# First norm of a two-layer hybrid block on one core: modulation in four blocks of 256 columns, rows of w_in loaded and split with them

## The chip, the cores and the metric

The kernel runs on one core of a Trainium2 chip, in float32, as one launch. The metric is the device time of that core in microseconds. The engines named below are TensorE (PE; its weight loads are listed as PEld), VectorE (DVE), ScalarE (ACT), GpSimd (POOL) and SyncE (SP), which issues most DMA transfers.

## The reference

One inference step of two layers over 128 context tokens and 256 latent tokens (384 together) of width 1024. Each layer modulates a normed input, feeds one wide input projection, mixes tokens in three branches (attention, gated linear attention, pooling), merges them and ends with a gated feed-forward part. What matters here is the start of the first layer:

```python
def _layer(x, cvec, p, ctx):
    mod = (jax.nn.silu(cvec) @ p['w_mod'] + p['b_mod']).reshape(-1, 1, 6 * D_MODEL)
    sh1, sc1, g1, sh2, sc2, g2 = jnp.split(mod, 6, axis=-1)
    hn = _rmsnorm(x, p['g_norm1']) * (1 + sc1) + sh1
    mix, new = _mixer(hn, p, ctx)          # begins with z = hn @ p['w_in']
    ...
```

`cvec` is one vector for the context tokens (c_ctx) and one for the latent tokens (c). The normed input `hn` can't be formed for a column before `sh1` and `sc1` of that column are known, and these need the first 2048 columns of `w_mod` (1024 x 6144): 8 MB.

## The kernel before, in words

All activations lie transposed: a tile `x[n]` holds channels 128 n to 128 n + 127 on the partitions and the 384 tokens along the row. `hn` is kept as two parts of reduced precision, `hh` and `hl`; each weight tile is likewise split into `wh` (a ScalarE copy, L151) and `wl` (a subtraction on VectorE, L155), and a product takes three matmuls, wh with hh, wh with hl, and wl with hh.

The order of work is written out by hand. `unit` (L100) lists every weight load; `seg` (L106) lists pieces of work with the units they use. `run` (L166) goes through the pieces, and before each one `pump` (L122) issues the next loads, strictly in the order of the list, as far as there is room: loads of w_mod go to tiles m0 to m5, m10 and m11 (each free again once its products are issued), loads of w_in to a ring of four tiles `raw`, free again once their split is done. `pump` also splits loaded tiles, in order, up to a limit `split_lim` and while fewer than three split pairs are held. The instructions of each engine run in the order in which they are issued.

`plan_start` (L331) writes the start of layer 0. It goes over n = 0 to 7, the eight column blocks of 128. For block n two loads of w_mod come, one for the shift columns and one for the scale columns (`w_cols`, L1178 to L1182: 1024 rows x 128 columns, runs of 512 B, 512 KB), and after block n + 1 the load of row n of w_in (`rows`, L1190 to L1195: 128 rows x 512 columns, 256 KB), so that rows 6 and 7 follow the last block. The stages s run from 0 to 9:

- `mod` (L350): 8 small matmuls for each of the two loads. The two conditioning vectors are the stationary operand (32 columns wide, of which two are used); four groups of 32 PSUM partitions each take two of the eight row blocks.
- `copy` (L359): ScalarE takes the partial sums out of PSUM. It also sets `split_lim`, so that row s - 1 may be split from stage s on.
- `post` for block s - 1: two transposes (L373), a sum over the four groups (L377), the bias (L380), the scale (L381), and `hn`: the modulated norm of that block. Even blocks do it on VectorE (L656), ScalarE (L674) and VectorE (L680), odd blocks on VectorE (L656), ScalarE (L664, L670) and POOL (L671).
- `row_fn` for row s - 2: twelve matmuls (L1242 to L1244) that add row block s - 2 of the product of w_in's 512 query and key columns of the gated branch. With row 7 come 32 small matmuls of the gate columns (L1231, weights `glw`) and the evacuations (L1246).

In between stand `bcast` (the norm's factor, L365, L367), `x_rest` (the last transposes of x, L322), `load_gl` (the load of `glw` on POOL's queue, L587), `prep_vec`, and in stage 6 `begin` (named `started_fn`): a POOL memset of a tile (L1200) and eight small loads of w_gate into it on SyncE (L1204). That tile is first used by the matmuls of L726, in the middle of the first tile of the next part. The next part (`tile_seg`, matmuls at L219) goes through the columns of w_in in tiles of 1024 x 128.

Of the kernel before, what the change touches and what calls it, by code (L numbers as in the profile page):

```python
# [10 lines left out]
AF = mybir.ActivationFunctionType  # L11
ALU = mybir.AluOpType
AX = mybir.AxisListType

D = 1024
KT = D // 128
# [11 lines left out]
V_BMOD, V_N1, V_N2, V_PS, V_GLA, V_QN, V_KN, V_BG, NV = 0, 48, 56, 64, 68, 69, 70, 71, 75  # L28


class Kern:
# [299 lines left out]
    def plan_start(self, rows, row_fn):  # L331

        nc, a = self.nc, self.a
        st = {}
        w_mod = a["w_mod"][0]
        um, ur = {}, {}
        for n in range(KT + 1):
            if n < KT:
                um[n] = [self.unit(("mod0", n, v), self.w_cols(w_mod, v * D + n * 128), 0,
                                   (0, 1, 2, 3, 4, 5, 10, 11)[(2 * n + v) % 8]) for v in range(2)]  # L340
            if n:
                ur[n - 1] = rows(n - 1)

        def mod(u, n, v):
            if v == 0:
                st[n] = self.psa()
            ps = st[n]
            for k in range(KT):
                j = k % 4
                nc.tensor.matmul(ps[32 * j:32 * j + 32, v * 128:v * 128 + 128], self.sc[:, k, :],  # L350
                                 self.raw[u][:, k * 128:k * 128 + 128], start=k < 4, stop=k >= 4,
                                 tile_position=(0, 32 * j))

        def copy(n):
            self.split_lim = ur[n - 1] + 1 if 0 < n <= KT else 0 if n == 0 else 1 << 30
            if n >= KT:
                return
            raw = self.t(("kn", "KA")[n % 2], [128, 256])
            nc.scalar.activation(raw, st[n][:, 0:256], AF.Copy)  # L359
            st[n] = raw  # L360

        def bcast():
            self.prep_vec(0, 0)
            ps = self.psa()
            nc.tensor.matmul(ps[:, 0:T], self.ones(), self.dg0)  # L365
            self.rs0 = self.t("ssq", [128, T])
            nc.vector.tensor_copy(self.rs0, ps[:, 0:T])  # L367

        def post(n):
            raw = st.pop(n)  # L370
            pt = self.psa()
            for v in range(2):
                nc.tensor.transpose(pt[:, v * 128:v * 128 + 128], raw[:, v * 128:v * 128 + 128], self.ident)  # L373
            m = self.modT[0]
            ab = m[:, n:n + 9:8, :]
            src = pt[:, 0:256].rearrange("p (v j c) -> p v c j", v=2, j=4)[:, :, 0:2, :]
            nc.vector.tensor_reduce(ab, src, axis=AX.X, op=ALU.add)  # L377
            vec = self.vec[0]
            bm = vec[:, V_BMOD + n:V_BMOD + n + 9:8]
            nc.vector.tensor_tensor(ab, ab, bm.unsqueeze(2).to_broadcast([128, 2, 2]), op=ALU.add)  # L380
            nc.vector.tensor_scalar(m[:, 8 + n], m[:, 8 + n], 1.0, vec[:, V_N1 + n:V_N1 + n + 1],  # L381
                                    op0=ALU.add, op1=ALU.mult)
            self.hn(0, n, 8, 0, self.rs0)

        self.modfin[0, 0] = self.modfin[0, 1] = iter(())
        for s in range(KT + 2):
            if s < KT:
                for v in range(2):
                    self.seg([um[s][v]], lambda u, s=s, v=v: mod(u, s, v), 0)
            self.seg([], lambda s=s: copy(s), 0)  # L390
            if s == 0:
                self.seg([], bcast, 0)
            if 1 <= s <= KT:
                self.seg([], lambda s=s: post(s - 1), 0)
            if s == 1:
                self.seg([], self.x_rest, 0)
            if s == 4:
                self.seg([], lambda: self.load_gl(0), 0)
            if s == 4:
                self.seg([], lambda: self.prep_vec(0, 1), 0)  # L400
            if s == 6:
                self.seg([], self.started_fn, 0)
            if s >= 2:
                self.seg([ur[s - 2]], lambda u, s=s: row_fn(u, s - 2))

    def setup(self):
        nc, a, t = self.nc, self.a, self.t
# [212 lines left out]
    def post(self, out, ps, rs, bb, scale=1.0):  # L620

        nc = self.nc
        nc.vector.tensor_scalar(bb, ps[:, T:T + 2], scale, None, op0=ALU.mult)
        nc.vector.scalar_tensor_tensor(out=out, in0=ps[:, 0:T], scalar=scale, in1=rs, op0=ALU.mult, op1=ALU.mult)  # L624

        def rest():
            for v, (c0, c1) in enumerate(SEG):
                nc.scalar.activation(out[:, c0:c1], out[:, c0:c1], AF.Identity, bias=bb[:, v:v + 1])
        return rest
# [554 lines left out]
    def plan_layer(self, l):  # L1184
        nc, a = self.nc, self.a
        st = {}
# [3 lines left out]
        def rows(k):  # L1190

            def dma(tl):
                ks = slice(k * 128, k * 128 + 128)
                nc.sync.dma_start(tl[:, 0:512], w_in[ks, C_QB:C_QB + 512])
            return self.unit((l, "row", k), dma, 512)  # L1195
# [19 lines left out]
        def row_fn(u, k):  # L1215
            if k == 0:
                st["z"] = [self.pd() for _ in range(3)] + [
                    self.psa(hold=True), self.psa(hold=True) if l else self.p("m")]
            if k == KT - 1:
                st["qbkb"] = self.mid(1, [128, 4, T])  # L1220
                st["q"] = self.mid(0, [128, 4, T])
            h, lo = self.wt[u]
            W = T + 2 if l else T
            hh, hl = (self.hhw, self.hlw) if l else (self.hh, self.hl)
            for g0 in (0, 4) if k == (2 if l else KT - 1) else ():

                ps = st["z"][0]
                for z, x in enumerate((hh, hl)):
                    for g in range(4):
                        kk = g0 + g  # L1230
                        nc.tensor.matmul(ps[32 * g:32 * g + 32, 0:W], self.glw[:, kk, :],  # L1231
                                         x[kk].bitcast(F32),
                                         start=kk == g and z == 0, stop=kk > g and z == 1, tile_position=(0, 32 * g))
            if k == KT - 1:
                if l:
                    bb = st["bb"]
                else:
                    nc.scalar.activation(st["gl"], st["z"][0][:, 0:T], AF.Copy)
            for i, c in enumerate((2, 3, 0, 1)):
                ps = st["z"][i + 1][:, 0:W]  # L1240
                cs = slice(c * 128, c * 128 + 128)
                nc.tensor.matmul(ps, h[:, cs], hh[k], start=k == 0, stop=False)  # L1242
                nc.tensor.matmul(ps, h[:, cs], hl[k], start=False, stop=False)
                nc.tensor.matmul(ps, lo[:, cs], hh[k], start=False, stop=k == KT - 1)  # L1244
                if k == KT - 1 and l == 0:
                    nc.scalar.activation(st["qbkb"][:, c, :], ps, AF.Copy, scale=0.125 if c < 2 else 1.0)  # L1246
                if i == 1:
                    if l and k == 2:
                        st["rs"] = next(st["norm"])
                    self.tick()  # L1250
                    self.run_low()
            if l:
                if k == 0:
                    st["norm"] = self.norm()
                    next(st["norm"])
                if k == 2:
                    begin()
                self.hn_after(k, 2, l, 8, 0, st.get("rs"))
                if k == 6:
                    st["bb"] = bb = self.t("rsmall", [128, 5, 2])  # L1260
                    st["rest"] = self.post(st["gl"], st["z"][0], st["rs"], bb[:, 4])
                if k == KT - 1:
                    st["rest"]()
                    for i, c in ((2, 0), (3, 1), (0, 2), (1, 3)):
                        self.post(st["qbkb"][:, c, :], st["z"][i + 1], st["rs"], bb[:, c], 0.125 if c < 2 else 1.0)()
            if k == KT - 1:
                if l:
                    self.sa_i = next(i for i in range(4) if i not in self.held and (i - 1) % 4 in self.held)
                self.held.clear()
                if l == 0:  # L1270
                    self.spawn(self.setup())
                st["gla"] = self.spawn(self.gla_all(l, st))
# [4 lines left out]
        else:  # L1277
            for k in range(KT):
                u = rows(k)
# [463 lines left out]
```

## Time and profile before

| | us |
|---|---|
| median of 3 runs | 1326.35 (1326.03 to 1326.6) |
| the profiled execution | 1326.22 |
| its span, first to last instruction | 1324.4 |
| TensorE busy | 1291.9 |
| VectorE busy | 852.9 |
| ScalarE busy | 596.1 |

The profile is of one execution. Times in it count from the start of its span; 1.8 us of the execution's time lie outside the span. The span is cut here at two places: until 43.27 us the loads of w_mod come in, and at 54.30 us the first matmul of L219 starts. A clock of 1.00 is the granted TensorE clock as a share of 2.4 GHz.

### The profile page before, as it was taken

The numbers are of one execution on the slowest core, as the hardware profiler recorded it, in microseconds if no ns is written. First come the engines' busy times: TensorE is split into PE (matmuls) and PEld (weight loads), VectorE is DVE, ScalarE is ACT, GpSimd is POOL, SyncE is SP. The second block draws the span as 40 slices with busy tenths as digits, with TensorE's granted clock in tenths as the row PEclk, the third lists the DMA queues.
The fourth block names the chain that finished last, engine by engine and source line by source line (L and its number), as shares of the span: only waits on it lengthen the run. The fifth ranks groups of instructions, "written<-read, shape, count | busy, mean of one in ns | idle before, by whom it ended". The sixth has DMA issues, their size and how long they took to land.

```text
span 1324.4 us, 23404 instructions
## 1 busy us (share of the span) xinstructions
PE 1291.9 (98%) x9285; PEld 1201.2 (91%) x9285; DVE 852.9 (64%) x1522; ACT 596.1 (45%) x1102; POOL 139.7 (11%) x190
## 2 busy tenths in 40 slices
PE   7999999999999999999999999999999999999998
PEld 5797788889998999999988887888999899999998
DVE  4497876454568768676877888754556787544432
ACT  5655455343366333333446646543435643333221
POOL 1142000010033000000222400001102300000000
PEclk9999999999999999999999999999999999999999
DMA  9943545556444656665645545355444266444442
GB/s 288 248 118 98 146 127 143 156 134 199 135 127 115 192 173 198 184 198 166 201 129 151 149 114 142 114 166 139 111 127 128 84 201 189 135 126 123 134 127 61
DMA packets 297788, 198.51 MB, mean 150 GB/s; under 512 B 24560, under 2 KB 282384, under 8 KB 297680
## 3 DMA queue, kind: packets, MB, share of 16 engines
q1 hardware_dynamic: 296928, 196.68, 52.7%
q8 instruction: 73, 1.20, 0.4%
q0 software_dynamic: 608, 0.28, 0.1%
q14 instruction: 35, 0.29, 0.1%
q10 hardware_dynamic: 144, 0.07, 0.0%
HBM read 194.64 MB, written 2.36 MB: 149 GB/s over the span
## 4 chain that ended last, share of the span: by engine, by line
PE 87%; DVE 6%; DMA 2%; issue 2%; SPq 1%; ACT 1%; POOL 1%; ACTq 0%; POOLq 0%; DVEq 0%
PE d L219 65%; PE d L1429 7%; PE d L1361 2%; DMA m<-in_w_mod_dram 2%; PE m L472 1%; PE s L1120 1%; PE s L1109 1%; PE s L1074 1%; DVE wl L155 1%; PE s L762 1%; DVE nm L1080 1%; PE s L949 1%; SPq L1181 1%; DVE ev L656 1%; PE s L943 1%
## 5 line engine op out<-in xcount | busy, mean ns | idle before, releaser
L155 DVE TENSOR_TENSOR wl<-raw,wh 128x1024 fp32r<-128x1024 f32 (+2 forms) x274 | 328.5, 1202 | 126.3 <-ACT wh L151 122.2
L151 ACT ACTIVATE wh<-raw 128x1024 fp32r<-128x1024 f32 (+2 forms) x276 | 280.0, 1017 | 172.6 <-PE d L219 63.6
L219 PE MATMUL d<-hl,wh 128*128 128x384 f32 x1248 | 252.9, 341 | 0.0
L219 PE MATMUL d<-hh,wh 128*128 128x384 f32 x1248 | 248.2, 342 | 2.0 <-DVE vf L624 2.0
L219 PE MATMUL d<-hh,wl 128*128 128x384 f32 x1248 | 243.0, 338 | 0.0
L219 PEld LDWEIGHTS d<-hh,wh 128*128 128x128 f32 x1248 | 216.0, 189 | 16.9 <-issue 10.9
L219 PEld LDWEIGHTS d<-hl,wh 128*128 128x128 f32 x1248 | 218.2, 189 | 2.0 <-issue 0.3
L219 PEld LDWEIGHTS d<-hh,wl 128*128 128x128 f32 x1248 | 219.8, 189 | 0.0
L219 PE MATMUL d<-m,wh 128*128 128x384 f32 x896 | 166.0, 337 | 0.0
L219 PEld LDWEIGHTS d<-m,wh 128*128 128x128 f32 x896 | 155.7, 188 | 0.4 <-issue 0.4
L251 ACT ACTIVATE m<-tt 128x384 fp32r<-128x384 f32 x60 | 31.3, 525 | 157.4 <-DVE tt L1531 125.7
L219 PE MATMUL d<-m,wl 128*128 128x384 f32 x448 | 87.5, 337 | 0.0
L219 PEld LDWEIGHTS d<-m,wl 128*128 128x128 f32 x448 | 78.6, 188 | 0.0
L1429 PE MATMUL d<-m,wh 128*128 128x384 f32 x384 | 72.2, 341 | 0.0
L1429 PEld LDWEIGHTS d<-m,wh 128*128 128x128 f32 x384 | 66.0, 188 | 6.6 <-issue 5.8
L710 DVE SCALAR_TENSOR_TENSOR x<-d,modT,x 128x128 f32<-128x128 f32 x64 | 23.6, 413 | 53.9 <-PE d L219 46.1
L1412 ACT ACTIVATE tt<-d 128x384 f32<-128x384 f32 x48 | 23.6, 491 | 72.4 <-PE d L219 62.5
L1449 POOL TENSOR_TENSOR m<-m,tt 128x384 f32<-128x384 f32 x16 | 16.9, 1081 | 368.7 <-DVE tt L1447 368.7
L561 POOL TENSOR_TENSOR ssq<-ssq,ev 128x384 f32<-128x384 f32 x18 | 29.4, 1636 | 248.9 <-ACT ev L559 248.9
L1531 DVE TENSOR_TENSOR tt<-tt,d 128x384 f32<-128x384 f32 x42 | 23.2, 554 | 48.9 <-PE d L219 48.6
L1518 ACT ACTIVATE tt<-d 128x384 f32<-128x384 f32 x42 | 20.6, 490 | 67.1 <-PE d L219 63.2
L1110 ACT ACTIVATE pT<-s 128x384 f32<-128x384 f32 (+1 forms) x48 | 20.1, 418 | 60.5 <-PE s L1109 60.5
(319 smaller groups left out, 1607.2 us busy)
## 6 DMA issues: line engine op xcount, KB each, us to landing
raw<-in_w_mod_dram SPq DMA_DIRECT2D x80, 512.0 KB, 3.8
raw<-in_w_in_dram SPq DMA_DIRECT2D x76, 512.0 KB, 4.0
raw<-in_w_ff_gate_dram SPq DMA_DIRECT2D x44, 512.0 KB, 4.8
raw<-in_w_ff_up_dram SPq DMA_DIRECT2D x44, 512.0 KB, 4.6
raw<-in_w_ff_down_dram SPq DMA_DIRECT2D x32, 448.0 KB, 4.4
m<-in_w_mod_dram SPq DMA_DIRECT2D x16, 512.0 KB, 7.1
raw<-in_w_in_dram SPq DMA_DIRECT2D x32, 256.0 KB, 3.9
raw<-in_w_out_dram SPq DMA_DIRECT2D x16, 512.0 KB, 4.0
```

What stands on the lines that cost most here:

```text
L151: nc.scalar.activation(h[:, f], w[:, f], AF.Copy)
L155: e.tensor_tensor(l[:, f], w[:, f], h[:, f].bitcast(F32), op=ALU.subtract)
L219: nc.tensor.matmul(ps, w[:, k * width + col:k * width + col + 128], xs[xi](k0 + k), start=first and n == 0, stop=last and n == tot - 1)
L251: self.nc.scalar.activation(h, v, AF.Copy)
L561: e.tensor_tensor(self.ssq, self.ssq, sq, op=ALU.add)
L710: nc.vector.scalar_tensor_tensor(out=self.x[n][:, c0:c1], in0=ps[:, c0:c1], scalar=self.modT[l][:, fg + n, v:v + 1], in1=self.x[n][:, c0:c ...
L1110: nc.scalar.activation(pTs[u // 2][:, v, 0:nk * 128], ps[:, 0:nk * 128], AF.Copy)
L1361: nc.tensor.matmul(vps[c], (self.hl if z else self.hh)[kk][:, c * 128:c * 128 + 128], w[:, k * 512:k * 512 + 512], start=kk == 0 and w is ...
L1412: nc.scalar.activation(tt, ps[:, 0:T], AF.Tanh, scale=0.5)
L1429: nc.tensor.matmul(ps[i], w[:, k * 256 + i * 128:k * 256 + i * 128 + 128], x2[xi](k), start=w is h and xi == 0 and k == 0, stop=w is lo an ...
L1518: nc.scalar.activation(tt, pg, AF.Tanh, scale=0.5)
L1531: nc.vector.tensor_tensor(tt, tt, pu, op=ALU.mult)
```

## The change

The eight column blocks of 128 become four of 256. For each block there are four loads of w_mod: shift and scale, each as the upper and the lower 512 rows, 512 rows x 256 columns (runs of 1 KB, 512 KB each as before). `mod` has four matmuls of 256 columns for each load. The rows of w_in come in pairs: for block 0 behind its fourth load, for the other blocks ahead of their fourth load. `split_lim` is set to include the pair of block s after the third load's products of that block, while the pair's own products come in stage s + 1. `copy` writes one tile of 512 columns. `post(s)` comes in its own stage s: four transposes, two reductions, one bias add and one scale over both column blocks, then `hn` twice. In stages 1 to 4 the products of row 2s - 2 come ahead of `post(s)` and those of row 2s - 1 behind it. `x_rest` moves into block 0, `load_gl` to stage 1, `prep_vec` to stage 2, `begin` to stage 3 (behind `post(3)`). The gate columns' products are done in two halves, with rows 5 and 7.

```diff
+        for s in range(NB):
+            def two_rows():
+                for n in (2 * s, 2 * s + 1):
+                    ur[n] = rows(n)
+            for i in range(4):
+                if s and i == 3:
+                    two_rows()
+                v, h = i // 2, i % 2
+                um[s, i] = self.unit(("mod0", s, i), self.w_cols(w_mod, v * D + s * 256, nk=4, k0=4 * h, width=256), 0,
+                                     (0, 1, 2, 3, 4, 5, 10, 11)[(4 * s + i) % 8])
+            if not s:
+                two_rows()
...
+            for j in range(4):
+                nc.tensor.matmul(ps[32 * j:32 * j + 32, v * 256:v * 256 + 256], self.sc[:, 4 * h + j, :],
+                                 self.raw[u][:, j * 256:j * 256 + 256], start=h == 0, stop=h == 1,
                                  tile_position=(0, 32 * j))
...
+            if s and i == 2:
+                self.split_lim = ur[2 * s + 1] + 1
...
+        def copy(s):
+            raw = self.t("pT", [128, 512], bufs=2)
+            nc.scalar.activation(raw, st[s], AF.Copy)
+            st[s] = raw
+            if s == 0:
+                self.split_lim = ur[1] + 1
...
+            for b in range(4):
+                nc.tensor.transpose(pt[:, b * 128:b * 128 + 128], raw[:, b * 128:b * 128 + 128], self.ident)
+            m, vec = self.modT[0], self.vec[0]
+            n = 2 * s
             for v in range(2):
...
+                src = pt[:, v * 256:v * 256 + 256].rearrange("p (h j c) -> p h c j", h=2, j=4)[:, :, 0:2, :]
+                nc.vector.tensor_reduce(m[:, 8 * v + n:8 * v + n + 2, :], src, axis=AX.X, op=ALU.add)
...
+            for h in range(2):
+                self.hn(0, n + h, 8, 0, self.rs0)
...
-        for s in range(KT + 2):
-            if s < KT:
-                for v in range(2):
-                    self.seg([um[s][v]], lambda u, s=s, v=v: mod(u, s, v), 0)
-            self.seg([], lambda s=s: copy(s), 0)
+        for s in range(NB + 1):
+            if s < NB:
+                for i in range(4):
+                    self.seg([um[s, i]], lambda u, s=s, i=i: mod(u, s, i), 0)
+                    if (s, i) == (0, 1):
+                        self.seg([], self.x_rest, 0)
+                self.seg([], lambda s=s: copy(s), 0)
             if s == 0:
                 self.seg([], bcast, 0)
-            if 1 <= s <= KT:
-                self.seg([], lambda s=s: post(s - 1), 0)
+            else:
+                self.seg([ur[2 * s - 2]], lambda u, s=s: row_fn(u, 2 * s - 2))
+            if s < NB:
+                self.seg([], lambda s=s: post(s), 0)
             if s == 1:
-                self.seg([], self.x_rest, 0)
-            if s == 4:
                 self.seg([], lambda: self.load_gl(0), 0)
-            if s == 4:
+            if s == 2:
                 self.seg([], lambda: self.prep_vec(0, 1), 0)
-            if s == 6:
+            if s == 3:
                 self.seg([], self.started_fn, 0)
-            if s >= 2:
-                self.seg([ur[s - 2]], lambda u, s=s: row_fn(u, s - 2))
+                self.seg([], free_split, 0)
+            if s:
+                self.seg([ur[2 * s - 1]], lambda u, s=s: row_fn(u, 2 * s - 1))
...
-            for g0 in (0, 4) if k == (2 if l else KT - 1) else ():
+            for g0 in ((0, 4) if l and k == 2 else (0,) if not l and k == 5 else (4,) if not l and k == KT - 1 else ()):
```

`free_split` sets `split_lim` to no limit.

## Rows read from the trace of the kernel before

**Rows 1.** The page: busy us, share of the span, instructions by engine.

```profile
PE 1291.9 (98%) x9285; PEld 1201.2 (91%) x9285; DVE 852.9 (64%) x1522; ACT 596.1 (45%) x1102; POOL 139.7 (11%) x190
```

**Rows 2.** Chain of waits at 35 us: start us, us, what.

```profile
34.85 8.38 DMA m<-in_w_mod_dram
...
43.27 0.65 PE s L350 x16
```

**Rows 3.** Waits, 8 to 52 us: engine, line waited for, total us, times, longest.

```profile
PE s L350 <- DMA m<-in_w_mod_dram: 6.1, 7, 1.8
```

**Rows 4.** Timeline of SyncE's issues: start us, us, queue, line, tiles, count.

```profile
36.50 2.57 SPq L1194 DMA_DIRECT2D raw<-in_w_in_dram  x2
...
43.28 5.39 SPq L1204 DMA_DIRECT2D m<-in_w_gate_dram  x8
```

**Rows 5.** Windows: length, busy PE PEld DVE ACT POOL, clock, DMA share, GB/s.

```profile
4.00:7.00 3.00, 1.64 (x8) 1.44 (x9) 0.01 (x1) 2.50 (x5) 2.34 (x13) 1.00 1.03 387
10.00:12.00 2.00, 1.30 (x21) 0.86 (x25) 1.05 (x4) 1.09 (x3) 0.00 (x0) 1.00 1.20 290
```

**Rows 6.** Timeline of TensorE after the last landing (and at 143 us).

```profile
43.84 0.44 PE L373 MATMUL s<-ident,kn 128*128 128x128 f32 x2
...
46.34 0.44 PE L1242 MATMUL d<-hh,wh 128*128 128x384 f32 x1
...
49.40 0.85 PE L1231 MATMUL d<-hh,glw 128*32 128x384 f32 x8
...
52.11 0.44 PE L1242 MATMUL d<-hh,wh 128*128 128x384 f32 x1
...
54.30 1.55 PE L219 MATMUL d<-hh,wh 128*128 128x384 f32 x8
...
56.38 1.46 PE L726 MATMUL s<-vf,m 128*128 128x384 f32 x4
...
143.37 0.64 PE L472 MATMUL m<-raw,sc 128*32 128x256 f32 x8
```

**Rows 7.** DMA issues, whole span: tile, queue, count, KB each, median us to landing.

```profile
raw<-in_w_in_dram SPq DMA_DIRECT2D x76, 512.0 KB, 4.0
...
raw<-in_w_br_c_dram SPq DMA_DIRECT2D x8, 512.0 KB, 3.4
```

**Rows 8.** Timeline of VectorE, post and norm of blocks 6 and 7.

```profile
44.32 0.17 DVE L377 TENSOR_REDUCE modT<-s 128x4 f32<-128x16 f32 x1 [3.10 <-PE s L373]
...
44.99 0.75 DVE L656 SCALAR_TENSOR_TENSOR ev<-x,modT,ssq 128x128 f32<-128x128 f32 x2
...
46.32 0.49 DVE L680 SCALAR_TENSOR_TENSOR hl<-ev,modT,hh 128x256 fp32r<-128x256 f32 x1 [0.16 <-ACT hh L674]
...
48.05 0.75 DVE L656 SCALAR_TENSOR_TENSOR ev<-x,modT,ssq 128x128 f32<-128x128 f32 x2
48.72 0.69 DVE L155 TENSOR_TENSOR wl<-raw,wh 128x512 fp32r<-128x512 f32 x1
```

**Rows 9.** Timeline of POOL, the memset of `begin` and block 7's subtraction.

```profile
42.73 0.52 POOL L1200 MEMSET m<- 128x512 f32 x1
49.98 1.01 POOL L671 TENSOR_TENSOR hl<-ev,hh 128x384 fp32r<-128x384 f32 x1 [6.73 <-ACT hh L670]
```

**Rows 10.** Line L1204 (both layers): issue ns min/median/max; landing us.

```profile
L1204 SPq DMA_DIRECT2D m<-in_w_gate_dram x16: 413/418/1459, 43.3 to 689.7; - x16
...
DMA to landing us min/median/max: 1.6/2.6/3.8
```

**Rows 11.** Windows, for the granted clock (the third number from the end).

```profile
22.00:26.00 4.00, 2.19 (x40) 1.48 (x39) 0.71 (x2) 1.35 (x4) 0.99 (x1) 1.00 1.16 310
...
157.80:161.20 3.40, 3.40 (x14) 3.40 (x13) 2.26 (x6) 2.16 (x7) 0.00 (x0) 0.53 0.21 35
```

**Rows 12.** Timeline of TensorE at 157 us.

```profile
157.39 0.55 PE L1109 MATMUL s<-ident,pr 128*128 128x128 f32 x3 [2.76 <-DVE Dg L838]
...
158.88 2.71 PE L219 MATMUL d<-hh,wl 128*128 128x384 f32 x8
```

More of the change, by code (lines that the diff above doesn't have):

```diff
@@ L333, in plan_start @@
         nc, a = self.nc, self.a
+        NB = KT // 2
         st = {}
@@ L336, in plan_start, with mod @@
         um, ur = {}, {}
[L337 to L351, printed above, removed]
-                                 tile_position=(0, 32 * j))
[L354 to L360, printed above, removed]
+        for s in range(NB):
[10 more added lines that the diff above has]
+                two_rows()
+        def mod(u, s, i):
+            v, h = i // 2, i % 2
+            if i == 0:
+                st[s] = self.psa()
+            ps = st[s]
+            for j in range(4):
+                nc.tensor.matmul(ps[32 * j:32 * j + 32, v * 256:v * 256 + 256], self.sc[:, 4 * h + j, :],
+                                 self.raw[u][:, j * 256:j * 256 + 256], start=h == 0, stop=h == 1,
+                                 tile_position=(0, 32 * j))
+            if s and i == 2:
[6 more added lines that the diff above has]
+                self.split_lim = ur[1] + 1
         def bcast():
@@ L367, in bcast, with post @@
             nc.vector.tensor_copy(self.rs0, ps[:, 0:T])
-        def post(n):
-            raw = st.pop(n)
+        def post(s):
+            raw = st.pop(s)
             pt = self.psa()
+            for b in range(4):
+                nc.tensor.transpose(pt[:, b * 128:b * 128 + 128], raw[:, b * 128:b * 128 + 128], self.ident)
+            m, vec = self.modT[0], self.vec[0]
+            n = 2 * s
             for v in range(2):
[L373 to L383, printed above, removed]
@@ L385, in plan_start @@
-        self.modfin[0, 0] = self.modfin[0, 1] = iter(())
-        for s in range(KT + 2):
-            if s < KT:
-                for v in range(2):
-                    self.seg([um[s][v]], lambda u, s=s, v=v: mod(u, s, v), 0)
-            self.seg([], lambda s=s: copy(s), 0)
+                src = pt[:, v * 256:v * 256 + 256].rearrange("p (h j c) -> p h c j", h=2, j=4)[:, :, 0:2, :]
+                nc.vector.tensor_reduce(m[:, 8 * v + n:8 * v + n + 2, :], src, axis=AX.X, op=ALU.add)
+            ab = m[:, 0:16, :].rearrange("p (v n) c -> p v n c", v=2)[:, :, n:n + 2, :]
@@ new lines, in post @@
+            bm = vec[:, V_BMOD:V_BMOD + 16].rearrange("p (v n) -> p v n", v=2)[:, :, n:n + 2]
+            nc.vector.tensor_tensor(ab, ab, bm.unsqueeze(3).to_broadcast([128, 2, 2, 2]), op=ALU.add)
+            nc.vector.scalar_tensor_tensor(
+                out=m[:, 8 + n:10 + n, :], in0=m[:, 8 + n:10 + n, :], scalar=1.0,
+                in1=vec[:, V_N1 + n:V_N1 + n + 2].unsqueeze(2).to_broadcast([128, 2, 2]), op0=ALU.add, op1=ALU.mult)
+            for h in range(2):
+                self.hn(0, n + h, 8, 0, self.rs0)
@@ L391, in plan_start, with free_split @@
+        def free_split():
+            self.split_lim = 1 << 30
+        self.modfin[0, 0] = self.modfin[0, 1] = iter(())
+        for s in range(NB + 1):
[5 more added lines that the diff above has]
+                self.seg([], lambda s=s: copy(s), 0)
             if s == 0:
                 self.seg([], bcast, 0)
-            if 1 <= s <= KT:
-                self.seg([], lambda s=s: post(s - 1), 0)
+            else:
+                self.seg([ur[2 * s - 2]], lambda u, s=s: row_fn(u, 2 * s - 2))
+            if s < NB:
+                self.seg([], lambda s=s: post(s), 0)
```

## The prediction, before the result

> **What bounds the kernel now.** I read the engine shares first. TensorE is busy 98% of the span [rows 1], so nearly everywhere else time is matmul time, and the change touches only the first 57 us. There the chain of waits says something else: from 34.85 to 43.23 us it runs through one transfer of w_mod, the second half of the eighth and last block, and only after it through TensorE [rows 2]. The waits say the same: TensorE waits seven times, 6.1 us in all, for blocks of w_mod [rows 3]. So the start is a stage bounded by transfers: 16 loads of w_mod of 512 KB, in runs of 512 B, and six of the eight 256 KB row loads of w_in (runs of 2 KB) pass in front of the last landing; the loads of rows 6 and 7 are issued behind it [rows 4]. The windows give the rates: 387 GB/s while x comes in runs of 4 KB, 290 GB/s once the 512 B runs have the queue [rows 5].
>
> After the last landing there is a tail bounded by TensorE, read from its timeline [rows 6]: from 43.27 to 54.30 us, 11.03 us, it does the products of the last half block (0.57), two pairs of transposes around row 5 (2.50 together, so 0.31 for the transposes, since a row takes 2.19), row 6 (3.06, of which 0.9 is waiting in its first matmuls), the gate products (2.71) and row 7 (2.19). From 54.30 on it is fed from tiles loaded ahead. What the change is worth is therefore: when does the last block land, and how much TensorE work stands behind it.
>
> **The landing.** All 16 blocks now come as 256 columns by 512 rows: the same 512 KB in 512 runs of 1 KB, not 1024 of 512 B. At 290 GB/s 512 KB take 1.81 us, at 387 GB/s 1.355 us [rows 5]. No row shows a long stretch of 1 KB runs. If the difference is a price per run, 1024 runs against 128, then 512 runs cost 1.355 + 0.453 x 384/896 = 1.55 us, 0.26 less than now. The first block comes right behind x in both versions, so 15 blocks count: -3.9 us. Bounds: nothing (runs of 1 KB cost the same per byte as 512 B) and 15 x 0.455 = -6.8 us (as cheap as 4 KB). A loss is excluded by the nearest row: a tile of w_br_c, in 1 KB runs, lands 3.4 us after its issue, one of w_in of the same size in 512 B runs after 4.0 [rows 7]. That row lies near the far bound, but for transfers that stand alone in the queue; for a full queue I take the middle value.
>
> Rows 6 and 7 of w_in now stand in front of the last quarter of the last block, because each block's two rows are put ahead of its fourth quarter. They are 512 KB in 256 runs, by the same line 1.42 us: +1.4 us on the landing. Sum: the last landing comes 2.5 us earlier, near 40.7.
>
> Row 7's load needs the slot of row 3, and so waits for row 3's subtraction on VectorE; the last quarter of w_mod is queued behind it on SyncE. With B the landing of the second block: products 0.57, row 0 2.19, then on VectorE up to the norm of column block 2 (1.55), that (1.8), the first operations of block 3 (0.75) and the subtraction (0.7) [rows 6, 8]: B + 7.6, or 2.8 more if the clock is at its lower level then. An idle queue lands a tile 4.0 us after issue [rows 7], row 7 in front of it takes 0.7: B + 12.3 to 15.1. The queue itself, with eight blocks and four rows ahead, gets there at B + 8 x 1.55 + 2.8 = B + 15.2. Covered, in the worst case just so.
>
> **The tail.** The number of products does not change, but their place does. Behind the last landing there now stand the products of a quarter of 256 columns (8 matmuls in 0.64 us where 16 of 128 columns took 0.65 [rows 2, 6]), four rows instead of three (rows 4 to 7), four transposes, and the gate products, split into halves before rows 5 and 7: 0.57 + 4 x 2.19 + 0.4 + 2.71 = 12.4 us, +1.4 us. What went: the 0.9 us in front of row 6; the norm of column block 6 ends at L + 6.1 (L is the landing; below), row 6 starts at L + 0.57 + 2 x 2.19 + 0.4 + 1.36 = L + 6.7. Second half of the gates: it needs the POOL subtraction of block 7 (L + 9.1) only in its last matmuls, at about L + 10. Evacuations, reductions and adds are fewer and larger, all on VectorE and ScalarE beside row products; I cost them at nothing. That only the even row of a pair is really split a block ahead (three split buffers, the odd one waits for a product to free one) costs nothing either: the odd one has a row and the transposes to cover it.
>
> **A wait that comes closer.** The first products of the gating branch (L726) use a tile that is cleared by a POOL memset and filled by eight small loads on SyncE. Before, the memset followed the POOL subtraction of block 5 and was over by 43.28 us, 13 us before its use at 56.38 [rows 4, 6, 9]. Now it is queued behind the subtraction of block 7. Worked out step by step [rows 6, 8, 9]: transposes at L + 2.76; first reduction 0.48 later plus 0.2 for two more transposes, L + 3.4; 0.67 plus 0.2 for a second reduction to the first norm operation, L + 4.3; the even block 44.99 to 46.81, 1.8, L + 6.1; the odd one 48.05 to 50.99, 2.9, L + 9.1; memset 0.5, L + 9.6. Eight issues at 0.42 + 0.04 us and a landing of 1.6 us [rows 10]: the eighth is issued at L + 12.8 and lands at L + 14.4. TensorE gets to L726 at L + 12.4 + 2.1 = L + 14.5. So just in time, 0; the other end, with the issues as slow as they were here (5.39 us for eight [rows 4], landing 2.6 [rows 10]), is L + 16.9, a wait of 2.4 us. I take 0, since the queue then holds one tile load at most.
>
> **Sum.** -3.9 + 1.4 + 1.4 + 0 = -1.1 us. The profiled execution took 1326.22 us for its span of 1324.4; that makes 1325.1, and the median lies 0.13 above the profiled one: **1325.2 us**. About 0.2%, 2.65 us, is what a measurement of this kernel can tell from no change; this is inside it.
>
> **The rivals.**
> - Cheap runs. If 1 KB runs go at the rate of the 4 KB ones, -6.8 + 1.35 + 1.4 = -4.0 us: 1322.3. For it: the 3.4 against 4.0 us [rows 7]. Against: that is one transfer at a time.
> - No cheaper runs. Then 0 + 1.4 + 1.4 = +2.8 us: 1329.1. Against it: 290 against 387 GB/s [rows 5]. The Trainium skill, "DMA: Bandwidth & Descriptors", section Specifications, speaks for it: it puts the least transfer for line rate at 512 B, and by that rule doubling the run buys nothing. The trace disagrees in so far as 512 B runs stay at 290 GB/s where 4 KB runs reach 387 [rows 5].
> - The late gate tile. At the far end of that chain TensorE stands 2.4 us in the middle of the first tile. A wait of 2.76 us that ended at 157.39 was followed by 3.4 us at a granted clock of 0.53, all but the 1.2 GHz level; eight matmuls took 2.71 us there and 1.55 elsewhere [rows 6, 11, 12], so some 1.6 us went in those 3.4. Together -1.1 + 2.4 + 1.6 = +2.9 us: 1329.2, slower. It decides from a wait of about 2 us on; below that it stays inside 0.2%.
> - A fall of the clock before the tail, if the pauses for transfers get longer: +1.6, still inside 0.2%. The pauses of up to 1.8 us between 22 and 26 us came with 1.00 [rows 3, 11]. With TensorE's work for a block near 7 us and a block's transfers at 4 x 1.55 + 1.4 = 7.6, the pauses there stay shorter than that; the long pause in front of the second block (no row product is due yet) is hidden by it.
>
> **How the numbers follow.** Forecast 51% (own range 1323.6 to 1328.0: half the gain per run more or less, a clock fall at most); cheap runs 25%; the late tile 14%; no cheaper runs 10%. Faster by over 0.2%: 25%; within: 51%; slower: 24%. The range goes to both outer cases with some 0.6 us beyond: 1321.8 to 1329.8.
>
> **What would show it.** In the changed profile: windows between 10 and 38 us near 338 GB/s (290: no cheaper runs; 380: cheap ones); the last block's products starting near 40.7 us; four rows behind them; L219 starting 12.4 us later, near 53.1; the first L726 with no idle time on TensorE ahead of it; clock 1.00 there. A landing after 42 us, or a wait of 2 us at L726, would make the forecast wrong.

## The result, and the profile after

After the change the kernel takes 1339.59 us (median of 4 runs, 1338.39 to 1340.05) where the kernel before took 1326.47 beside it: ratio 1.0094, 95% interval [1.0081, 1.0107], so 13.1 us slower. The forecast was 1325.2 us, and the range ended at 1329.8. The profiled execution took 1339.57 us, its span 1337.6 against 1324.4.

The stage that the prediction worked out is not where the 13.1 us went. TensorE's timeline of the changed kernel answers to [rows 6] (start us, us, line, out<-in, count, idle before). L357 is `mod`, L1259 a row's first matmul, L381 the transposes, L1248 the gate columns, L743 is what was L726:

```profile
23.04 1.08 PE L357 MATMUL s<-m,sc 128*32 128x256 f32 x8 [2.24 <-DMA m<-in_w_mod_dram]
...
39.97 0.64 PE L357 MATMUL s<-m,sc 128*32 128x256 f32 x8 [0.97 <-DMA m<-in_w_mod_dram]
40.54 0.44 PE L1259 MATMUL d<-hh,wh 128*128 128x384 f32 x1
...
42.75 0.60 PE L381 MATMUL s<-ident,pT 128*128 128x128 f32 x4
43.28 0.85 PE L1248 MATMUL d<-hh,glw 128*32 128x384 f32 x8
...
44.71 0.44 PE L1259 MATMUL d<-hh,wh 128*128 128x384 f32 x1
...
52.77 1.57 PE L219 MATMUL d<-hh,wh 128*128 128x384 f32 x8
54.18 0.87 PE L219 MATMUL d<-hl,wh 128*128 128x384 f32 x4
54.89 1.45 PE L743 MATMUL s<-vf,m 128*128 128x384 f32 x4
```

The products of the last block's last load start at 39.97 us (forecast 40.7), four rows stand behind them, L219 starts at 52.77 (forecast 53.1; before 54.30) and L743 has no idle time ahead of it. So at 52.77 us the changed kernel is 1.5 us ahead, and at the end it is 13.2 behind. The page's first line, which answers to [rows 1], says on which engine: TensorE is busy 13.8 us longer, with 128 matmuls fewer.

```profile
PE 1305.7 (98%) x9157; PEld 1213.3 (91%) x9157; DVE 853.8 (64%) x1514; ACT 595.9 (45%) x1098; POOL 136.8 (10%) x190
```

Grouping L219 by operand tiles (duration min/median/max, first and last start in us) shows where. Before:

```profile
L219 PE MATMUL d<-hh,wh x1248: 332/337/633, 54.3 to 1221.9; 128*128 128x384 f32 x179
...
L219 PE MATMUL d<-m,wl x448: 335/337/339, 371.2 to 1318.5; 128*128 128x384 f32 x150
```

After:

```profile
L219 PE MATMUL d<-hh,wh x1248: 334/337/634, 52.8 to 1233.7; 128*128 128x384 f32 x179
...
L219 PE MATMUL d<-m,wl x448: 336/337/345, 371.9 to 1331.8; 128*128 128x384 f32 x150
```

The median duration of one product is 337 ns in both: matmuls overlap, and a duration doesn't show how fast they follow each other. The starts do: from the first to the last of them 1264.2 us before, 1279.0 after, 14.8 us more for the same products. A plain stretch of them shows it at close range, before:

```profile
70.53 1.55 PE L219 MATMUL d<-hh,wh 128*128 128x384 f32 x8
...
81.63 1.55 PE L219 MATMUL d<-hh,wl 128*128 128x384 f32 x8
```

and after:

```profile
70.56 1.57 PE L219 MATMUL d<-hl,wh 128*128 128x384 f32 x8
...
80.40 1.56 PE L219 MATMUL d<-hh,wl 128*128 128x384 f32 x8
```

Before, 64 products lie between the two starts: 11.10 / 64 = 0.1734 us each. After, 56 products: 9.84 / 56 = 0.1757. Over all pairs of neighbours in the trace (some 5,400) the mean from start to start is 173.3 ns before and 176.0 after; after, the spacings repeat, in most of the trace every five products (173, 174, 175, 182, 176 ns), in the stretch shown every three (174, 175, 178). There are 5,664 such products (L219 and the feed-forward part's L1446): 5,664 x 2.7 = 15 us, the size of the whole loss. The granted clock is 1.00 in both stretches.

The clock has a small part in it all the same. In the window from 800 to 820 us (length, busy PE PEld DVE ACT POOL, clock, DMA share, GB/s) it is 1.00 before and 0.91 after:

```profile
800.00:820.00 20.00, 16.93 (x214) 13.07 (x214) 16.03 (x44) 12.72 (x32) 0.00 (x0) 1.00 0.47 132
```

```profile
800.00:820.00 20.00, 17.12 (x190) 13.43 (x191) 15.92 (x42) 11.54 (x29) 0.00 (x0) 0.91 0.45 134
```

That is worth up to 0.09 x 20 = 1.8 us. b_hh64wh192, a run of experiment 3 with the slow pace and a clock of 1.00 in this window, takes 1277.6 us from first to last L219, 13.4 more than before: so most of the 14.8 us belongs to the pace.

**What the change moved without naming it.** A tile's place in SBUF (its first byte within each partition, read here from the compiled program) follows from the order in which the program first names the tiles. `copy(0)` now names `pT` at the very start (6,144 bytes), ahead of `kn`, `vec0`, `ev`, `ssq` and `KA` (11,072 bytes), and so `wh` starts at byte 161792 and not 166720, `wl` at 174080 and not 179008. `hh`, `hl`, `raw` and m0 to m11 stay. Taken modulo 256 bytes, the weights moved from 64 to 0. The moving operands (the activations that a product streams past its weights: hh, hl and some of the m tiles) stand at 128 in both.

### The profile page after: what moved, and what is told of

The parts are those of the page before. It is cut to its first block, busy times and chain, and to the rows that moved or that the text cites. A ratio compares the mean times of both kernels' runs of the same rounds, so it can differ in the third digit from the quotient of the medians.

```text
span 1337.6 us, 23133 instructions
## 1 busy us (share of the span) xinstructions
PE 1305.7 (98%) x9157; PEld 1213.3 (91%) x9157; DVE 853.8 (64%) x1514; ACT 595.9 (45%) x1098; POOL 136.8 (10%) x190
## 4 chain that ended last, share of the span: by engine, by line
PE 88%; DVE 6%; DMA 2%; issue 2%; ACT 1%; POOL 1%; SPq 0%; ACTq 0%; POOLq 0%; DVEq 0%
PE d L219 65%; PE d L1446 7%; PE d L1378 2%; DMA m<-in_w_mod_dram 2%; PE m L489 1%; PE s L1137 1%; PE s L1126 1%; DVE wl L155 1%; PE s L1091 1%; PE s L779 1%; DVE nm L1097 1%; PE s L966 1%; DVE ev L673 1%; PE s L960 1%; PE d L233 1%
## 5 line engine op out<-in xcount | busy, mean ns | idle before, releaser
L219 PE MATMUL d<-hl,wh 128*128 128x384 f32 x1248 | 255.8, 342 | 0.0
L219 PE MATMUL d<-hh,wh 128*128 128x384 f32 x1248 | 251.5, 343 | 2.0 <-DVE vf L641 2.0
L219 PE MATMUL d<-hh,wl 128*128 128x384 f32 x1248 | 246.1, 339 | 0.0
L219 PEld LDWEIGHTS d<-hh,wh 128*128 128x128 f32 x1248 | 218.8, 188 | 17.0 <-issue 10.9
L219 PEld LDWEIGHTS d<-hl,wh 128*128 128x128 f32 x1248 | 220.9, 189 | 2.0 <-issue 0.3
L219 PEld LDWEIGHTS d<-hh,wl 128*128 128x128 f32 x1248 | 222.6, 189 | 0.0
L219 PE MATMUL d<-m,wh 128*128 128x384 f32 x896 | 168.2, 339 | 0.0
L219 PEld LDWEIGHTS d<-m,wh 128*128 128x128 f32 x896 | 157.7, 188 | 0.4 <-issue 0.4
L219 PE MATMUL d<-m,wl 128*128 128x384 f32 x448 | 88.5, 338 | 0.0
L219 PEld LDWEIGHTS d<-m,wl 128*128 128x128 f32 x448 | 79.6, 188 | 0.0
L1446 PE MATMUL d<-m,wh 128*128 128x384 f32 x384 | 73.1, 342 | 0.0
L1446 PEld LDWEIGHTS d<-m,wh 128*128 128x128 f32 x384 | 66.7, 188 | 6.6 <-issue 5.8
L578 POOL TENSOR_TENSOR ssq<-ssq,ev 128x384 f32<-128x384 f32 x18 | 26.6, 1479 | 255.6 <-ACT ev L576 255.6
```

The lines of the kernel that those rows point to most:

```text
L219: nc.tensor.matmul(ps, w[:, k * width + col:k * width + col + 128], xs[xi](k0 + k), start=first and n == 0, stop=last and n == tot - 1)
L578: e.tensor_tensor(self.ssq, self.ssq, sq, op=ALU.add)
L1446: nc.tensor.matmul(ps[i], w[:, k * 256 + i * 128:k * 256 + i * 128 + 128], x2[xi](k), start=w is h and xi == 0 and k == 0, stop=w is lo an ...
```

## The experiments

Each was run beside the kernel before on the same chip; ratios are to that kernel. The runs were spread over several chips, so two runs are best compared by their ratios. "Pace" is the mean from start to start of the products with wh and wl, out of the trace's start times.

**1. The places alone, taken out of the change and put into the old kernel.** a_old is the changed kernel, with the tiles from `kn` on named once, at the end of `head`, in the old order; b_new is the kernel before, with the same tiles named there in the new order. The list shown is that of a_old.

```diff
+        for tag, n, *b in (('kn', 384), ('vec0', 75), ('ev', 384, 4), ('ssq', 384), ('KA', 384), ('wh', 1024, 3), ('wl', 1024, 3), ...
+            self.t(tag, [128, n], bufs=b[0] if b else 1)
```

Expected of a_old: 

> The changed kernel, with every tile placed in SBUF where the kernel before has it (tiles named once at the start in the old order; no instruction added). Theory 'place' (TensorE's products with wh or wl as weights go 1.5% slower because the change moved wh and wl in SBUF): matmuls of 384 columns back at 173.3 ns from start to start, start of the stage as in the changed kernel (first L219 matmul near 52.8 us instead of 54.3), total 1.5 us under the kernel before, 1325. Theory 'program' (the slower pace comes from the changed instruction stream, wherever the tiles lie): stays near 176 ns and 1339.6. Theory 'chip' (the changed kernel was timed on a slower chip): the kernel before, beside it, is slow too.

Expected of b_new: 

> The kernel before, with every tile placed where the changed kernel has it. Place: pace 176 ns, near 1340.5 to 1341 us (13.1 + 1.5 us over 1326.4). Program: 173.3 ns and 1326.4.

a_old: 1324.70 us, ratio 0.998 [0.9971, 0.9988], pace 173.3. b_new: 1340.06 us, ratio 1.0096 [1.0081, 1.0112], pace 176.0, L219 at 54.22 as before. The loss follows the places and not the new order of work; without it the change gains 1.6 to 3.8 us (the interval of its ratio, times 1327).

**2. Is it wh and wl, and not another tile that moved?** An unused tile of a few bytes is put in front of the tile that is to be shifted; nothing else changes. b_pad192 (before) brings wh, wl to 0 modulo 256, a_pad320 (after) brings them back to 64.

```diff
+                    if "pad" not in self.__dict__:
+                        self.pad = self.t("pad", [128, 48])      # a_pad320: 80
                     h = self.t("wh", [128, 1024], F32R, bufs=self.HB)
```

Expected of b_pad192: 

> The kernel before, with an unused 192 B ahead of wh alone, so that wh and wl (and what lies behind them) start at a multiple of 512 B, as in the changed kernel, and not 320 B past one. Place, by alignment to 512 B: 176 ns, near 1340.5. Place, by which region of SBUF: 173.3 ns, 1326.4. Program: 1326.4.

Expected of a_pad320: 

> The changed kernel, with an unused 320 B ahead of wh, so that wh and wl start 320 B past a multiple of 512 B, as in the kernel before; pT stays in front of them. Place, by alignment: 173.3 ns and near 1325. Place, by region: 176 ns and 1339.6. Program: 1339.6.

b_pad192: 1339.75 us, ratio 1.0093 [1.0079, 1.0107], pace 176.0. a_pad320: 1324.89 us, ratio 0.9979 [0.997, 0.9988], pace 173.4. One pad of 192 bytes in the old kernel costs as much as the whole change.

b_padwl puts the 192 bytes between wh and wl, so that wl alone (and what follows) moves; b_padglw puts them behind wl; b_whonly moves wh to 0 and keeps wl at 64 (192 bytes ahead of wh, 64 ahead of wl).

Expected of b_padwl: 

> The kernel before with 192 B ahead of wl alone: wl at multiples of 512 B, wh where it was. If each matmul's own weights decide: only the products with wl (a third) go at 176 ns, some 4.4 us more, near 1331. If wh alone decides: 1327. If what lies behind wl decides: the whole 13 us.

Expected of b_padglw: 

> The kernel before with 192 B ahead of glw, behind wh and wl: all tiles behind them move, wh and wl don't. If the weights' place decides: 173.3 ns, near 1327. If the tiles behind decide: near 1340.

Expected of b_whonly: 

> The kernel before with wh at multiples of 256 B and wl 64 B past one, the counterpart of the run that moved wl alone (1331.9). If each matmul's own weights decide: products with wh (two of three) at 176 ns, those with wl at 173.3, near 1326.5 + 8.9 = 1335. If the last loaded of the two decides, another split.

b_padwl: 1331.91 us, ratio 1.0043 [1.0023, 1.0064]. Its timeline of TensorE (here L221 is what was L219) shows the slow products among the others: from the start of the wl group to the next 1.41 us, of the wh groups 1.39.

```profile
70.44 1.55 PE L221 MATMUL d<-hh,wh 128*128 128x384 f32 x8
71.83 1.55 PE L221 MATMUL d<-hl,wh 128*128 128x384 f32 x8
73.22 1.57 PE L221 MATMUL d<-hh,wl 128*128 128x384 f32 x8
74.63 1.55 PE L221 MATMUL d<-hh,wh 128*128 128x384 f32 x8
```

b_padglw: 1327.22 us, ratio 1.0002 [0.9991, 1.0013], pace 173.3. b_whonly: 1335.47 us, ratio 1.007 [1.005, 1.009]; 176.0 ns with wh (175.5 to 176.5 ns by the moving operand), 173.0 with wl. A product is slow when its own weight tile stands badly, whatever the other one does.

**3. What is a bad place?** First theory: weights at a multiple of 256 (or of 512) bytes. b_pad64 and b_pad448 are the pad of experiment 2 with 64 and 448 bytes: weights at 128 and at 0 modulo 256 (384 and 256 modulo 512).

Expected of b_pad64: 

> The kernel before with 64 B ahead of wh: wh and wl start 384 B past a multiple of 512 B (a multiple of 128 B, not of 256). Slow from multiples of 128 B on: 176 ns, near 1340. Slow only at multiples of 256 or 512 B: 173.3 ns, near 1327.

Expected of b_pad448: 

> The kernel before with 448 B ahead of wh: wh and wl start 256 B past a multiple of 512 B. Slow at multiples of 128 or 256 B: near 1340. Slow only where a block of 128 weights begins exactly at a multiple of 512 B: near 1327.

b_pad64: 1326.93 us, ratio 1.0002 [0.999, 1.0013], pace 173.6 to 173.9. b_pad448: 1340.23 us, ratio 1.0106 [1.0075, 1.0136], pace 176.0. So 256 is the period that counts, not 512. Then the moving operands were shifted too, by a pad in front of `hh` (it shifts hh, hl, the m tiles, raw and all tiles behind them); b_hh0wh0 brings the moving operands and the weights to 0, b_hh0wh128 and b_hh64wh192 keep the distance of the changed kernel at other places.

```diff
+        if "pad0" not in self.__dict__:
+            self.pad0 = self.t("pad0", [128, 32])    # b_hh64wh192: 48
         hh, hl = (t(n, [128, HW], F32R) for n in ("hh", "hl"))
...
+                        self.pad = self.t("pad", [128, 16])    # the other two: 48
                     h = self.t("wh", [128, 1024], F32R, bufs=self.HB)
```

Expected of b_hh0wh0: 

> The kernel before with 128 B ahead of hh and 64 B ahead of wh: hh, hl, m4, m5, wh and wl all start at multiples of 256 B (elsewhere hh, hl, m4 and m5 lie 128 B past one). If the place of the weights by itself decides: products with wh or wl at 176 ns, near 1340, and the 512-column products, whose weights are hh, slower too (233 ns now). If the distance between weights and moving operand decides (128 B apart modulo 256 in all slow runs so far): 173.3 ns and 1326.5.

Expected of b_hh0wh128: 

> Before, with hh, hl, the m tiles and raw moved to starts that are multiples of 256 bytes in their partition and wh, wl to 128 past one. So the distance from moving operand to weights is 128 modulo 256, as in the kernel after, while neither stands where it stood there. If the distance decides: 176.0 ns from start to start of a 384-column product, L219's first product near 49.4 us as with the tiles at (0, 0), and 1324.4 + 13 = about 1337.5 us. If the slow pair is weights at 0 with moving at 128 and no other: 173.3 to 174.1 ns and 1322 to 1325 us.

Expected of b_hh64wh192: 

> Before, with hh, hl, the m tiles and raw at 64 past a multiple of 256 bytes and wh, wl at 192 past one: distance 128 again, from a third pair of places. If the distance decides: 176.0 ns and, by where the loads land, 1333 to 1340 us; if the pair (weights 0, moving 128) alone is slow: 173.3 to 174.1 ns and 1321 to 1327 us. For the loads: if only a multiple of 256 is the cheap start of a destination, the windows of the w_mod loads show 290 GB/s and L219 starts near 54.3 as before; if every start but 128 past is cheap, 347 GB/s and near 49.4.

b_hh0wh0: 1324.39 us, ratio 0.9983 [0.9973, 0.9994], pace 173.5 to 173.9, with the weights at multiples of 256: the first theory fell. On its timeline 40 products take 6.93 us, 0.1733 each:

```profile
69.73 1.55 PE L221 MATMUL d<-hh,wh 128*128 128x384 f32 x8
...
76.66 1.55 PE L221 MATMUL d<-hh,wl 128*128 128x384 f32 x8
```

b_hh0wh128: 1335.21 us, ratio 1.0062 [1.0047, 1.0077], pace 176.0. b_hh64wh192: 1340.34 us, ratio 1.0094 [1.0079, 1.0109], pace 176.0. In all pairs of places that were tried (multiples of 64 bytes), what decides is the distance between the weights and the moving operand, modulo 256:

| weights - moving | (moving, weights) tried | ns per product |
|---|---|---|
| 192 | (128, 64), (0, 192) | 173.3 to 173.4 |
| 0 | (128, 128), (0, 0) | 173.5 to 173.9 |
| 64 | (0, 64), the m products of b_m0 below | 174.5 to 174.6 |
| 128 | (128, 0), (0, 128), (64, 192) | 175.8 to 176.2 |

b_hh64wh192's timeline has the same pace as that of the changed kernel, 8.43 us for 48 products, 0.1756 each:

```profile
71.12 1.56 PE L221 MATMUL d<-hh,wh 128*128 128x384 f32 x8
...
79.55 1.56 PE L221 MATMUL d<-hh,wh 128*128 128x384 f32 x8
```

Why this distance costs was not tried: that a weight load reads SBUF beside the running product and that the two collide there would fit, and is only argued.

b_hh0wh128 stayed 2.3 us under its forecast, though its L219 starts at 50.60 and not 49.4. The forecast was worked out from b_hh0wh0, and that run's profile has the clock lower between 800 and 820 us. b_hh0wh0 and then b_hh0wh128:

```profile
800.00:820.00 20.00, 16.97 (x111) 14.00 (x108) 13.59 (x40) 11.01 (x25) 0.00 (x0) 0.83 0.40 114
```

```profile
800.00:820.00 20.00, 17.11 (x201) 13.60 (x201) 17.31 (x47) 11.02 (x26) 0.00 (x0) 1.00 0.51 154
```

0.17 x 20 = 3.4 us: from first to last L219 b_hh0wh128 takes 9.9 us more than b_hh0wh0 (1277.5 against 1267.6), and with these 3.4 us the difference is the 13 us expected.

**4. The price of the runs.** a_runs512 is a_old with each 512 KB load of the first layer's start as two loads of 128 columns, so in runs of 512 B again (and twice as many loads of half the size). a_rowslast is a_old with rows 6 and 7 loaded behind the last block (and split after `copy(3)`).

```diff
+            def dma(tl):
+                d3 = tl.rearrange("p (k c) -> p k c", k=4)
+                for c in (0, 128):
+                    nc.sync.dma_start(d3[:, :, c:c + 128], w_mod[k0 * 128:k0 * 128 + 512, c0 + c:c0 + c + 128].rearrange("(k p) c -> p k c", p=128))
```

```diff
-                if s and i == 3:
+                if s in (1, 2) and i == 3:
                     two_rows()
...
-            if not s:
+            if s in (0, 3):
                 two_rows()
```

Expected of a_runs512: 

> The changed kernel with every tile where the kernel before has it (1324.7 us), and each 512 KB load of w_mod issued as two loads of 128 columns, in runs of 512 B; order and amount of the loads unchanged. If runs of 1 KB save 0.26 us on each of 15 blocks, as predicted: the last block lands 3.9 us later and the total is 3.9 us more, near 1328.6. If they save nothing: 1324.7.

Expected of a_rowslast: 

> The same kernel (tiles where the kernel before has them, runs of 1 KB), with the loads of rows 6 and 7 behind the last block's fourth load, and their split behind copy(3). If the two rows cost the landing 1.4 us, as predicted: the last block lands 1.4 us earlier and the total is near 1323.3. If the tail then waits for the rows or their split instead: 1324.7 or more.

a_runs512: 1331.54 us, ratio 1.004 [1.0028, 1.0052]. That is 6.8 us over a_old's median, and over the forecast of 1328.6, but not all of it is the loads': the profiled execution, with a mean granted clock of 0.994, took 1327.98 us, the other six, at 0.989 to 0.992, 1330.99 to 1333.69 (a_old's eleven: 0.992 to 0.995). The two profiled executions differ by 5.4 us, 5.3 of it by the first L219 (57.35 against 52.03). Its windows are back at the rate of [rows 5] (length, busy PE PEld DVE ACT POOL, clock, DMA share, GB/s), and the products of its last load, on the timeline, wait for it until 44.64:

```profile
10.00:12.00 2.00, 0.73 (x12) 0.31 (x16) 1.09 (x5) 1.16 (x4) 0.00 (x0) 1.00 1.20 291
```

```profile
44.64 0.64 PE L366 MATMUL s<-m,sc 128*32 128x256 f32 x8 [2.17 <-DMA m<-in_w_mod_dram]
```

The kernel before reached the same rate with half as many loads of twice the size [rows 5], so the number of loads doesn't show in it. The changed kernel, whose loads go to the same places, had:

```profile
10.00:12.00 2.00, 1.16 (x17) 0.30 (x10) 1.10 (x5) 1.17 (x4) 0.00 (x0) 1.00 1.10 348
22.00:26.00 4.00, 2.96 (x14) 2.15 (x15) 1.18 (x2) 2.29 (x5) 1.00 (x1) 0.57 1.10 349
```

a_rowslast: 1324.30 us, ratio 0.9981 [0.9972, 0.9991]; a_old had 0.998, so nothing is told apart by the time. The timelines say why (L359 is `mod`, and the window is a_old's). a_old and then a_rowslast:

```profile
37.72 2.24 PE L359 MATMUL s<-m,sc 128*32 128x256 f32 x32
39.89 0.45 PE L1261 MATMUL d<-hh,wh 128*128 128x384 f32 x1
...
52.03 1.55 PE L219 MATMUL d<-hh,wh 128*128 128x384 f32 x8
```

```profile
22.00:26.00 4.00, 2.53 (x13) 1.72 (x14) 1.08 (x1) 2.07 (x4) 1.00 (x1) 0.50 1.10 349
```

```profile
37.77 1.93 PE L359 MATMUL s<-m,sc 128*32 128x256 f32 x32
```

The 32 products of the last block run without a wait for a load in a_rowslast; in a_old they take 0.31 us more, so it waits at most that long. By the time that TensorE gets to the last block it has landed, or nearly so, and TensorE itself is the bound. It stood at a granted clock of 0.50 from 22 to 26 us in both, during and after a wait of 1.9 (a_old) or 2.2 us for the last load of the second block. What the two rows cost the landing can't show in such a start beyond 0.3 us.

**5. The place where a load lands.** b_hh0wh0 started L219 5 us early (49.34) though its loads were those of before. b_m0 moves the tiles that loads go to (m0 to m8, m10, m11, raw) to multiples of 256 bytes by a pad of 128 bytes in front of them, and a second one ahead of wh leaves hh, hl, wh and wl at 128 and 64 (the small tiles between the two pads, such as sc, kn and ev, move by 128 with the others); a_hh0 is a_old with the pad of 128 bytes in front of `hh`, so the tiles that loads go to stand at 0 and the distance is 192.

```diff
+        if "pad0" not in self.__dict__:
+            self.pad0 = self.t("pad0", [128, 32])
         self.xraw = [self.mid(6 + c, [128, 1024]) for c in range(3)]
...
+                        self.pad = self.t("pad", [128, 32])
                     h = self.t("wh", [128, 1024], F32R, bufs=self.HB)
```

Expected of b_m0: 

> Before, with the destinations of the loads alone (m0 to m11, raw) moved by 128 to multiples of 256 bytes; hh, hl, wh, wl keep their places modulo 256 (128 and 64). If the destination's start sets the rate of the loads: 347 to 366 GB/s in the windows from 10 us on, L219's first product near 49.3 and not 54.30, and 1326.5 - 5 = about 1321.5 us, if the products with m (distance now 64) keep 173.3 ns. If the hh tiles' move was what shortened the start: 290 GB/s, 54.3 and 1326.5 us.

Expected of a_hh0: 

> After, with the order of the tiles of before (as a_old) and hh, hl, the m tiles and raw moved by 128 to multiples of 256 bytes; wh, wl stand 192 past one, so the distance is 192, as in the kernel before. Expected by the theory of the distance: 173.3 ns. By the theory that the destination's start sets the rate of the loads: if the 512 KB loads of 256 columns gain as the 128-column ones did (290 to 347 GB/s), 350 to 366 GB/s becomes 385 or so, L219's first product comes 1 to 3 us ahead of a_old's 52.03, and the time is 1321 to 1324 us; if the two gains are one and the same limit, the rate stays at 350 to 366 and the time is 1324.7 us.

b_m0: 1324.59 us, ratio 0.9982 [0.9972, 0.9992]. Its windows and its first L219:

```profile
10.00:12.00 2.00, 1.26 (x33) 0.76 (x28) 1.21 (x5) 1.31 (x5) 0.00 (x0) 1.00 1.15 347
12.00:14.00 2.00, 1.52 (x19) 0.68 (x18) 0.78 (x2) 0.34 (x1) 0.00 (x0) 1.00 1.15 364
```

```profile
48.95 1.55 PE L221 MATMUL d<-hh,wh 128*128 128x384 f32 x8
```

So the same 512 B runs go at 347 and not 290 GB/s [rows 5], and L219 comes 5.35 us earlier. That it is the destination, and not one of the small tiles that move with it, is the plain reading; it was not tried apart. The products with m, now at distance 64, give back 1,920 x 1.2 = 2.3 us; -5.35 + 2.3 = -3.05, and the span is 3.2 shorter (the forecast of 1321.5 left this pace out). b_hh64wh192, with the destinations at 64, shows the old rate (296 GB/s in the same window) and L219 at 54.74: of the starts tried, 64 and 128 are dear, 0 is cheap.

a_hh0: 1323.02 us, ratio 0.9963 [0.995, 0.9976], pace 173.4. Its median is the lowest of all that were run, below that of both kernels; its interval overlaps a_old's, so the times alone don't show that it beats a_old.

```profile
10.00:12.00 2.00, 1.36 (x19) 0.49 (x12) 1.34 (x7) 1.44 (x4) 0.00 (x0) 1.00 1.09 386
...
24.00:26.00 2.00, 2.00 (x8) 2.00 (x7) 0.00 (x0) 0.00 (x0) 0.00 (x0) 0.50 1.08 395
```

```profile
35.82 1.93 PE L361 MATMUL s<-m,sc 128*32 128x256 f32 x32
...
49.82 1.55 PE L219 MATMUL d<-hh,wh 128*128 128x384 f32 x8
```

Both gains add: 386 GB/s, the rate of the 4 KB runs of x [rows 5]. L219 comes only 2.2 us ahead of a_old: the last block's products wait for no load here either, so TensorE, and not the transfers, ends the start.

## Why the prediction was wrong

**The step that failed** is the sum's silent last line: that "the change touches only the first 57 us" and that from 54.30 on TensorE "is fed from tiles loaded ahead", so that what comes after moves as a whole and keeps its length. It did not: +14.8 us (first to last L219), as 5,664 products went from 173.3 to 176.0 ns. The evacuation into `pT` was costed "at nothing", by its time on ScalarE; its cost is that it names a tile early and shifts wh and wl by 4,928 bytes. No rival held this, and none could have given +13 us. Of the two signs that the prediction named for being wrong, a landing after 42 us and a wait of 2 us at L726, neither came. Experiments 1 and 2 show the cause, experiment 3 its rule; why the chip has that rule stays open.

**The landing.** -2.5 us was forecast, -3.3 came (39.97 against 43.27). Its first term was too small: -3.9 by 0.26 us a load, from an assumed price per run. With 512 B runs in the new order the last load's products start at 44.64 (a_runs512), with 1 KB runs at 39.97: -4.7. The rate was 348 GB/s and more, not 338; at 355 a load takes 1.48 us, 0.33 less than at 290, and 15 x 0.33 = 5.0. The second term, +1.4 for rows 6 and 7, fits where transfers bound: 44.64 - 43.27 = 1.37 with the same run length as before (one comparison, and a_rowslast couldn't test it). The Trainium skill, "DMA: Bandwidth & Descriptors", section Specifications, puts the least transfer for line rate at 512 B. The runs disagree for destinations at 128 modulo 256 (290 GB/s at 512 B, 348 at 1 KB) and still for those at 0 (347 and 386).

**The tail.** 12.4 us forecast, 12.8 measured (39.97 to 52.77). The four transposes took 0.53 and not 0.4 us, the gate products as two halves 2.85 and not 2.71, a row 2.21 and not 2.19, its products with wh and wl being slow there too.

**The gate tile.** Worked out step by step, and it came as forecast: no wait. The eight issues, on the timeline of SyncE's queue, and the memset on that of POOL:

```profile
49.24 3.58 SPq L1221 DMA_DIRECT2D m<-in_w_gate_dram  x8
```

```profile
48.69 0.53 POOL L1217 MEMSET m<- 128x512 f32 x1
```

The last issue ends at 52.82, 12.85 us behind the landing (forecast 12.8). A landing is counted from the start of its issue: this one starts near 52.4 and lands 1.7 us later, near 54.1; TensorE comes at 54.89. The forecast counted from the end of the issue, and so saw 0.1 us to spare where there are 0.8.

**The rivals.** The price of the runs (-4.7) came out between the forecast (-3.9) and "cheap runs" (-6.8), nearer the forecast; "no cheaper runs" and "the late gate tile" did not come. The fall of the clock came, and twice: 0.50 from 15.8 to 19.2 us, and 0.57 from 22 to 26 (against 1.00 in [rows 11]), the second in a wait of 2.24 us for the last load of the second block: the argument that pauses get shorter did not hold for that one. In the changed kernel neither cost the landing anything, since the last block still waited 0.97 us for its load; in a_old and a_hh0, whose clock fell there too, TensorE was the bound. What their start takes at a clock of 1.00 was not run.

Had the tiles kept their places, the same change gains 1.6 to 3.8 us (a_old). Its direction is that of the sum, -1.1; with the run term at -4.7 the sum is -1.9, inside that interval.

## What to carry to other kernels

In a kernel like this one a new tile, or an old one named earlier, shifts tiles behind it; where matmuls fill the time, compare the places of weights and moving operands modulo 256 bytes before and after any edit, for a shift can cost more than the edit is worth (13 us here, against 1.6 to 3.8). Read the pace of pipelined matmuls from start to start: their durations had the same median of 337 ns at both paces. A cost of "nothing" needs an answer for memory as well as for time.

## What the runs showed of the hardware that was not expected

- A 128 x 128 weight load and its 384-column product go at 173.3 ns from start to start or at 176.0, by the distance of weights and moving operand in SBUF modulo 256 bytes (128: slow; 192 and 0: fast; 64: between; only multiples of 64 were tried). That is 1.5% of a product and 13 us of this kernel. In most of the trace the slow pace comes above all from one product in five, at 182 ns, not from a longer time of each.
- Loads whose destination starts at a multiple of 256 bytes in its partition went faster than those 64 or 128 past one: 347 GB/s against 296 (64) and 290 (128) in runs of 512 B, 386 against 348 (128) in runs of 1 KB, each in the window from 10 to 12 us.
